# The last product of a down part, made in two matmuls of 256 columns

## The chip, the cores and the metric

The kernel runs on one core of a Trainium2 chip. The metric is device time in microseconds (us) of one execution. Engines are named as in the profile: PE is the matmul engine and PEld its loading of weights, DVE the vector engine, ACT the scalar engine, POOL GpSimd, SP the engine that issues most transfers.

## The reference

One decoder layer on 256 rows of 1024 columns in float32: a norm, attention with 16 heads of 64, a projection, a second norm, a gated feed-forward block with a causal convolution of width 3 (D_FF = 2816), a last norm. The change sits in the feed-forward block:

```python
def conv_ffn(y, w_up, conv_w, conv_b, w_down):
    u = y @ w_up
    u = causal_depthwise_conv(u, conv_w) + conv_b      # width 3, cut short here
    gate, val = jnp.split(u, 2, axis=-1)
    return (jax.nn.silu(gate) * val) @ w_down
```

## The kernel before, in words

Every float32 matrix is split in a high and a low part, `whi` (made by ACT, line 141) and `wlo` (made by DVE, line 154), and each product is made as three: high x high, low x high, high x low. All matmuls of these products go through one helper, `mm` on line 73, so the profile shows one line for them and tells them apart by their tiles.

The feed-forward block works on 22 tiles of 128 hidden columns. **An up tile** (`up`, `up_k`) makes 128 gate and 128 value columns for all 256 rows: 2 x 8 x 3 = 48 matmuls with a weight tile as the stationary operand and 256 columns of `yt` moving, written to a tile named `bank`. `gates` then reads the bank on DVE (line 540), runs the convolution and the gate on ACT and DVE, and leaves `at`, the 128 hidden columns split in high and low. **A down part** (`down`) multiplies two finished `at` tiles with 256 rows of `w_down`: `rows_product` is called for `kk` = 0 and 1, and each call goes over two halves of the rows (`t`), three products (`n`) and two halves of the output columns, 12 matmuls with `at` as the stationary operand and 512 columns of the weight moving. They add into four accumulators named `acc`, which stay open over all parts.

The order on PE is the order in which the code is written (the schedule is manual). From up tile 3 on, each odd up tile is followed by a down part, so PE runs 24 matmuls of 512 columns, then 96 of 256 (two up tiles), and so on. There are eight such down parts (0 to 7); after the last of them four up tiles follow, 192 matmuls. The three down parts that are left (`TAIL`) come after all up tiles; at the very end their last output columns are made in two banks of 256 columns (lines 642 to 649), with `at` stationary as in the other down parts.

```python
    def down(i, chains, whole=False):
        ...
        for kk in range(2):
            k = 2 * i + kk
            rows_product(accs, at[k], ("d", i), kk, chains, k == 0, ...)
```

The splits into `whi` and `wlo` run ahead of PE by a set number of pieces (`split_to`, `AHEAD`); DVE and ACT share their time between them and `gates`.

Of the kernel before, what the change touches and what calls it, by code (L numbers as in the profile page):

```python
# [16 lines left out]
NT = S // P  # L17
# [6 lines left out]
NF = F // P  # L24
# [14 lines left out]
def bucket_of(d):  # L39
    exact = BUCKETS // 2  # L40
    if d < exact:
        return d
    big = exact + int(math.log(d / exact) / math.log(MAX_DIST / exact) * (BUCKETS - exact))
    return min(big, BUCKETS - 1)
# [3 lines left out]
def tile_block(ctx: ExitStack, tc, x, attn_norm, w_qkv, w_o, rel_bias, ffn_norm, w_up, conv_w,  # L48
# [14 lines left out]
    def acc():  # L63
        return psA.tile([P, 512], F32, name="acc")
# [7 lines left out]
    def mm(o, lhsT, rhs, start, stop):  # L72
        nc.tensor.matmul(o, lhsT, rhs, start=start, stop=stop, skip_group_check=True)  # L73
# [92 lines left out]
    def split_to(g, ahead=0):  # L166
        n = 2 * (place[g] + 1) + ahead
        unit(max(0, n - state["lo"]))
# [114 lines left out]
    while d1 >= 0:  # L283
        b = bucket_of(d1)
# [3 lines left out]
        n = d1 - d0 + 1  # L288
# [12 lines left out]
    rk, rq = (ap.tile([P, S], F32, name=n) for n in ("rk", "rq"))  # L301
    nc.vector.memset(stat[:, 1, :], 0.0)

    def rows_product(accs, lhs, g, kk, chains, start, stop):

        for t in range(NT):
            halves = [half for half in range(2) if (t, half) in chains]
            a_hi, a_lo = (lhs[:, i, t * P:(t + 1) * P] for i in range(2))
            for n, (a, w) in enumerate(((a_hi, hi), (a_lo, hi), (a_hi, lo))):
                for half in halves:  # L310
                    mm(accs[t, half], a, w[g, kk][:, half * 512:(half + 1) * 512],
                       start and n == 0, (stop is True or stop == (t, half)) and n == 2)

    CHAINS = [(t, half) for t in range(NT) for half in range(2)]
    accs = {c: acc() for c in CHAINS}
# [3 lines left out]
    for i in range(4):  # L319
        if i < 3:  # L320
            transposed(2 * i + 2, g1)
        for kk in range(2):
            k = 2 * i + kk
            rows_product(accs, yt[:, :, k, :], ("v", i), kk, CHAINS, k == 0, k == KD - 1)
        unit(2)
        if i == 1:
            nc.scalar.activation(junk[0], xt[0], AF.Square, accum_out=stat[:, 0, 0:1])
        if i == 2:
            nc.scalar.activation(junk[1], xt[1], AF.Square, accum_out=stat[:, 0, 1:2])
            r1 = rstds()  # L330
            d1 = diagonals(r1)
# [119 lines left out]
    accs = {}  # L451

    def o_part(t, half, ks):
        if (t, half) not in accs:
            accs[t, half] = acc()
        for k in ks:
            split_to(("o", k // 2))
            rows_product(accs, ot[:, :, k, :], ("o", k // 2), k % 2, [(t, half)], k == 0, k == KD - 1)
# [50 lines left out]
    at = {}  # L509
    accs = {}  # L510
# [54 lines left out]
    def down(i, chains, whole=False):  # L565
        split_to(("d", i))
        for c in chains:
            if c not in accs:
                accs[c] = acc()
        for kk in range(2):  # L570
            k = 2 * i + kk
            rows_product(accs, at[k], ("d", i), kk, chains, k == 0, k == NF - 1 or (CHAINS[3] if whole and kk else False))

    first = [up_ps() for _ in range(2)]
    up_k(0, first[0], range(0, 4))
# [9 lines left out]
    for j in range(NF):  # L585
        if j < 2:
            gates(j, first[j])
        else:
            up(j)
        if j == 4:  # L590
            nc.scalar.activation(gf, gf, AF.Copy, scale=math.sqrt(D))
        split_to(("up", j), AHEAD if j < 8 else AHEAD + 2)
        i = (j - 3) // 2
        if j >= 3 and j % 2 == 1 and i < first_tail:
            down(i, CHAINS, i == first_tail - 1)
            split_to(("d", i), AHEAD if j < 8 else AHEAD + 2)
# [34 lines left out]
    for i in range(first_tail, NG - 1):  # L631
        down(i, CHAINS[:2])
    left, right = slice(0, 512), slice(512, D)
    down(NG - 1, [(0, 0)])
    add_part(0, left, 3, accs[0, 0])
    down(NG - 1, [(0, 1)])
# [44 lines left out]
```

## Time and profile before

| | |
|---|---|
| time, median of 3 runs | 319.25 us (319.23 to 319.75) |
| time of the profiled execution | 319.19 us |
| its span in the trace | 317.4 us |
| PE busy | 306.6 us (97%), 2142 matmuls |
| weight loads (PEld) | 280.9 us (89%) |
| DVE, ACT, POOL busy | 243.0, 180.2, 17.3 us |

The span runs from the first to the last instruction in the trace; the 1.8 us between it and the time lie around it. A busy PE in the profile is not a PE at its peak: matmuls overlap, and what the next one adds to the time is the distance from start to start, which the text calls the step of a matmul.

### The profile page before, as it was taken

To read this page: it belongs to the slowest core of one execution; us is meant where nothing else is said; L and a number is where in the kernel's file an instruction comes from. 1 tells how busy PE (TensorE), PEld (TensorE's weight loads), DVE (VectorE), ACT (ScalarE), POOL (GpSimd) and SP (SyncE) were. 2 spreads that over 40 slices of the span, in tenths; PEclk is the share of its full clock that TensorE was granted. 3 is DMA by queue.
4 is the path that set the end of the run, shared out by engine and by line. 5 is a ranking of instruction groups with operands and counts; after the bars stand their busy time and mean duration, and the time that the engine had idled before them with its cause. 6 is when DMAs were issued, how large, how long until landed. Compare 5 with 4: busy or idle time off the path is not lost.

```text
span 317.4 us, 5462 instructions
## 1 busy us (share of the span) xinstructions
PE 306.6 (97%) x2142; PEld 280.9 (89%) x2142; DVE 243.0 (77%) x460; ACT 180.2 (57%) x322; POOL 17.3 (5%) x55
## 2 busy tenths in 40 slices
PE   7999998999999999999999999999999999999992
PEld 7788998988888788999998989898989999999881
DVE  2475888888888595599988695989595959599662
ACT  4675576555556684557656464757272727366221
POOL 4602000000000000000000000000000000000000
PEclk9999999999999999999999999999999999999998
DMA  7997396718442356247476556567374747500011
GB/s 243 417 379 234 103 328 187 276 24 265 144 122 95 121 146 250 70 142 255 139 262 201 197 157 240 191 213 261 132 267 132 259 140 221 177 0 2 0 68 66
DMA packets 38902, 56.58 MB, mean 178 GB/s; under 512 B 1164, under 2 KB 32604, under 8 KB 38876
## 3 DMA queue, kind: packets, MB, share of 16 engines
q1 hardware_dynamic: 37724, 53.05, 49.0%
q0 software_dynamic: 848, 2.65, 3.1%
q10 hardware_dynamic: 304, 0.53, 0.4%
q8 instruction: 17, 0.28, 0.3%
q14 instruction: 9, 0.07, 0.1%
HBM read 55.15 MB, written 1.07 MB: 177 GB/s over the span
## 4 chain that ended last, share of the span: by engine, by line
PE 72%; ACT 9%; DVE 9%; issue 5%; DMA 3%; SPq 1%; POOLq 0%; POOL 0%; DVEq 0%; ACTq 0%
PE bank L73 41%; PE acc L73 29%; ACT sc L395 4%; DMA raw<-in_w_qkv_dram 3%; DVE sc L386 3%; ACT whi L141 2%; DVE wlo L154 2%; ACT ot L427 1%; ACT pt L411 1%; DVE pt L412 1%; DVE ot L429 1%; PE twobank L73 1%; DVE xs L608 0%; PE bank L258 0%; SPq L184 0%
## 5 line engine op out<-in xcount | busy, mean ns | idle before, releaser
L73 PE MATMUL bank<-yt,whi 128*128 128x256 f32 x720 | 127.1, 280 | 0.1
L154 DVE TENSOR_TENSOR wlo<-raw,whi 128x1024 fp32r<-128x1024 f32 x98 | 117.1, 1219 | 1.2 <-ACT whi L141 1.1
L73 PEld LDWEIGHTS bank<-yt,whi 128*128 128x128 f32 x720 | 110.2, 188 | 1.1 <-ACT yt L260 0.5
L73 PE MATMUL bank<-yt,wlo 128*128 128x256 f32 x360 | 100.8, 280 | 0.0
L141 ACT ACTIVATE whi<-raw 128x1024 fp32r<-128x1024 f32 x98 | 98.7, 1049 | 3.6 <-DMA raw<-in_w_qkv_dram 3.6
L73 PEld LDWEIGHTS bank<-yt,wlo 128*128 128x128 f32 x360 | 68.8, 191 | 0.0
L544 ACT ACTIVATE cv<-u,params 128x256 f32<-128x256 f32 x44 | 24.2, 598 | 69.0 <-DVE u L540 69.0
L73 PE MATMUL acc<-whi,at 128*128 128x512 f32 x164 | 44.7, 389 | 0.0
L73 PE MATMUL acc<-yt,whi 128*128 128x256 f32 x224 | 40.3, 283 | 0.0
L73 PEld LDWEIGHTS acc<-yt,whi 128*128 128x128 f32 x224 | 33.8, 188 | 2.4 <-issue 2.3
L73 PEld LDWEIGHTS acc<-whi,at 128*128 128x128 f32 x164 | 30.1, 188 | 5.7
L540 DVE TENSOR_TENSOR u<-bank,rb 128x512 f32<-128x512 f32 x22 | 15.2, 690 | 24.5 <-PE bank L73 24.4
L73 PE MATMUL acc<-yt,wlo 128*128 128x256 f32 x112 | 31.0, 277 | 0.0
L73 PE MATMUL acc<-wlo,at 128*128 128x512 f32 x82 | 26.1, 389 | 0.0
L395 ACT ACTIVATE sc<-sc,nm 128x128 f32<-128x128 f32 (+1 forms) x32 | 14.3, 448 | 19.2 <-DVE nm L390 19.2
L556 DVE SCALAR_TENSOR_TENSOR cv<-u,params,cv 128x254 f32<-128x254 f32 x44 | 21.3, 483 | 1.6
L554 DVE SCALAR_TENSOR_TENSOR cv<-u,params,cv 128x255 f32<-128x255 f32 x44 | 21.1, 479 | 0.3 <-ACT cv L544 0.3
L73 PEld LDWEIGHTS acc<-yt,wlo 128*128 128x128 f32 x112 | 21.0, 188 | 0.0
L73 PE MATMUL acc<-whi,ot 128*128 128x512 f32 x64 | 20.4, 397 | 0.4 <-DVE ot L429 0.4
L73 PEld LDWEIGHTS acc<-wlo,at 128*128 128x128 f32 x82 | 15.4, 188 | 3.2
L73 PE MATMUL acc<-whi,yt 128*128 128x512 f32 x64 | 17.6, 396 | 0.0
L73 PEld LDWEIGHTS acc<-whi,ot 128*128 128x128 f32 x64 | 11.6, 188 | 3.0 <-DVE ot L429 0.7
(119 smaller groups left out, 306.5 us busy)
## 6 DMA issues: line engine op xcount, KB each, us to landing
raw<-in_w_up_dram SPq DMA_DIRECT2D x22, 1024.0 KB, 5.1
raw<-in_w_qkv_dram SPq DMA_DIRECT2D x11, 1024.0 KB, 8.4
raw<-in_w_down_dram SPq DMA_DIRECT2D x11, 1024.0 KB, 4.9
raw<-in_w_o_dram SPq DMA_DIRECT2D x4, 1024.0 KB, 7.0
bias<-line_d POOLq DMA_DIRECT2D x8, 256.0 KB, 5.0
raw<-in_w_qkv_dram SPq DMA_DIRECT2D x2, 512.0 KB
xs<-in_x_dram SPq DMA_DIRECT2D x2, 256.0 KB
xs<-in_x_dram SPq DMA_DIRECT2D x1, 512.0 KB
```

Source lines behind the costliest of these rows:

```text
L73: nc.tensor.matmul(o, lhsT, rhs, start=start, stop=stop, skip_group_check=True)
L141: nc.scalar.activation(h, src, AF.Copy)
L154: nc.vector.tensor_tensor(l, src, h, op=ALU.subtract)
L386: nc.vector.tensor_tensor_reduce(out=sc[p][:, a, c], in0=ps[:, c], in1=bias[p][:, a, b], op0=ALU.add, op1=ALU.max, scale=1.0, scalar=-3.0e ...
L395: nc.scalar.activation(sc[p][:, a, c], sc[p][:, a, c], AF.Exp, bias=nm[:, j], accum_out=z[:, j])
L411: nc.scalar.activation(pt[p][:, 0, :], ps[:, :768], AF.Copy)
L412: nc.vector.tensor_tensor(pt[p][:, 1, :], ps[:, :768], pt[p][:, 0, :].bitcast(F32), op=ALU.subtract)
L427: nc.scalar.activation(h, o, AF.Copy)
L540: nc.vector.tensor_tensor(u, ps, rb2.unsqueeze(1).to_broadcast([P, 2, S]), op=ALU.mult)
L544: nc.scalar.activation(c[:, a, :], u[:, a, :], AF.Identity, scale=w2, bias=b)
L554: nc.vector.scalar_tensor_tensor(c[:, a, 1:], u[:, a, :S - 1], w1, c[:, a, 1:], op0=ALU.mult, op1=ALU.add)
L556: nc.vector.scalar_tensor_tensor(c[:, a, 2:], u[:, a, :S - 2], w0, c[:, a, 2:], op0=ALU.mult, op1=ALU.add)
```

## The change

`rows_product` gets an argument `border`. Where it is set, the last matmul of the call (second half of the rows, third product, second half of the output columns) is made as two matmuls of 256 columns, into the two halves of the same 512 columns of the accumulator, with the same stationary operand. `down` sets it for `kk` = 1 of the parts that make all four chains, which are the parts 0 to 7.

```diff
-    def rows_product(accs, lhs, g, kk, chains, start, stop):
+    def rows_product(accs, lhs, g, kk, chains, start, stop, border=False):
...
             for n, (a, w) in enumerate(((a_hi, hi), (a_lo, hi), (a_hi, lo))):
                 for half in halves:
-                    mm(accs[t, half], a, w[g, kk][:, half * 512:(half + 1) * 512],
-                       start and n == 0, (stop is True or stop == (t, half)) and n == 2)
+                    pieces = 2 if border and (t, n, half) == (NT - 1, 2, halves[-1]) else 1
+                    size = 512 // pieces
+                    for b in range(0, 512, size):
+                        mm(accs[t, half][:, b:b + size], a, w[g, kk][:, half * 512 + b:half * 512 + b + size],
+                           start and n == 0, (stop is True or stop == (t, half)) and n == 2)
...
-            rows_product(accs, at[k], ("d", i), kk, chains, k == 0, k == NF - 1 or (CHAINS[3] if whole and kk else False))
+            rows_product(accs, at[k], ("d", i), kk, chains, k == 0,
+                         k == NF - 1 or (CHAINS[3] if whole and kk else False), kk == 1 and chains == CHAINS)
```

On PE the end of down part 0 and the start of up tile 4 stand like this before (the names are output <- operands; `acc` marks the down part, `bank` the up tile; 128x256 and 128x512 are the outputs):

```order
L73 MATMUL acc<-whi,at 128x512 x4
L73 MATMUL acc<-wlo,at 128x512 x2
L73 MATMUL bank<-yt,whi 128x256 x2
L73 MATMUL bank<-yt,wlo 128x256
L73 MATMUL bank<-yt,whi 128x256 x2
```

And the same place in the changed kernel:

```order
L73 MATMUL acc<-whi,at 128x512 x4
L73 MATMUL acc<-wlo,at 128x512
L73 MATMUL acc<-wlo,at 128x256 x2
L73 MATMUL bank<-yt,whi 128x256 x2
L73 MATMUL bank<-yt,wlo 128x256
L73 MATMUL bank<-yt,whi 128x256 x2
```

The second of the two matmuls with `wlo` has become two of half the width, so the matmul ahead of the up tile has 256 columns where it had 512. The other seven places read alike; nothing else moves on PE, and the orders of DVE, ACT, POOL and SP are as before.

## Rows read from the trace of the kernel before

**Rows 1.** The page: busy time of the engines; PE and its granted clock in 40 slices of the span, in tenths; the chain that ended last, by line.

```profile
PE 306.6 (97%) x2142; PEld 280.9 (89%) x2142; DVE 243.0 (77%) x460; ACT 180.2 (57%) x322; POOL 17.3 (5%) x55
...
PE   7999998999999999999999999999999999999992
...
PEclk9999999999999999999999999999999999999998
...
PE bank L73 41%; PE acc L73 29%; ACT sc L395 4%; DMA raw<-in_w_qkv_dram 3%; DVE sc L386 3%; ACT whi L141 2%; DVE wlo L154 2%; ACT ot L427 1%; ACT pt L411 1%; DVE pt L412 1%; DVE ot L429 1%; PE twobank L73 1%; DVE xs L608 0%; PE bank L258 0%; SPq L184 0%
```

**Rows 2.** The chain that ended last, in order of time, in the feed-forward block: start in us, length in us, what, and how many instructions. `bank` pieces are up tiles, `acc` pieces down parts.

```profile
129.79 5.46 PE bank L73 x48
135.69 13.61 PE bank L73 x120
149.30 5.46 PE acc L73 x24
154.76 11.31 PE bank L73 x96
166.07 5.44 PE acc L73 x24
171.50 11.31 PE bank L73 x96
182.81 5.44 PE acc L73 x24
...
255.24 11.31 PE bank L73 x96
266.55 5.44 PE acc L73 x24
271.99 22.61 PE bank L73 x192
294.60 6.81 PE acc L73 x30
```

**Rows 3.** PE's instructions in order of time at the end of up tile 3 and the start of down part 0: start in us, time from the first start to the last end in us, engine, line, operation, output <- operands, shapes, how many of a kind in a row.

```profile
148.69 0.28 PE L73 MATMUL bank<-yt,wlo 128*128 128x256 f32 x1
148.80 0.39 PE L73 MATMUL bank<-yt,whi 128*128 128x256 f32 x2
149.03 0.28 PE L73 MATMUL bank<-yt,wlo 128*128 128x256 f32 x1
149.14 1.08 PE L73 MATMUL acc<-whi,at 128*128 128x512 f32 x4
150.06 0.62 PE L73 MATMUL acc<-wlo,at 128*128 128x512 f32 x2
```

**Rows 4.** The same view at the end of down part 0 and the start of up tile 4.

```profile
154.14 0.62 PE L73 MATMUL acc<-wlo,at 128*128 128x512 f32 x2
154.60 0.40 PE L73 MATMUL bank<-yt,whi 128*128 128x256 f32 x2
154.83 0.28 PE L73 MATMUL bank<-yt,wlo 128*128 128x256 f32 x1
154.95 0.40 PE L73 MATMUL bank<-yt,whi 128*128 128x256 f32 x2
155.19 0.28 PE L73 MATMUL bank<-yt,wlo 128*128 128x256 f32 x1
```

**Rows 5.** The same view at two other places where a run of 256-column matmuls begins: after the spread of the row factors (128-column matmuls into `acc`, ahead of the rest of up tile 1), and in attention after the scores (`bank<-kt,qt`).

```profile
135.19 0.50 PE L73 MATMUL acc<-diag,ones 128*128 128x128 f32 x3
135.44 0.48 PE L73 MATMUL bank<-yt,whi 128*128 128x256 f32 x2
135.77 0.28 PE L73 MATMUL bank<-yt,wlo 128*128 128x256 f32 x1
135.88 0.39 PE L73 MATMUL bank<-yt,whi 128*128 128x256 f32 x2
136.11 0.28 PE L73 MATMUL bank<-yt,wlo 128*128 128x256 f32 x1
...
57.78 0.50 PE L73 MATMUL acc<-yt,whi 128*128 128x256 f32 x2
58.12 0.29 PE L73 MATMUL acc<-yt,wlo 128*128 128x256 f32 x1
58.24 0.39 PE L73 MATMUL acc<-yt,whi 128*128 128x256 f32 x2
58.48 0.28 PE L73 MATMUL acc<-yt,wlo 128*128 128x256 f32 x1
58.59 0.39 PE L73 MATMUL acc<-yt,whi 128*128 128x256 f32 x2
58.81 0.28 PE L73 MATMUL acc<-yt,wlo 128*128 128x256 f32 x1
```

**Rows 6.** The same view near the end of the program, where the last output columns of the down parts go into a bank of 256 columns.

```profile
306.45 0.39 PE L73 MATMUL acc<-wlo,at 128*128 128x512 f32 x1
306.68 0.40 PE L73 MATMUL bank<-whi,at 128*128 128x256 f32 x2
306.91 0.28 PE L73 MATMUL bank<-wlo,at 128*128 128x256 f32 x1
307.03 0.40 PE L73 MATMUL bank<-whi,at 128*128 128x256 f32 x2
307.27 0.28 PE L73 MATMUL bank<-wlo,at 128*128 128x256 f32 x1
```

**Rows 7.** Busy time of each engine (and its instructions) in one stretch of 16.70 us, one down part and two up tiles, with granted clock, share of the DMA engines and GB/s; and who waited for whom between 155 and 306 us (us in total, times, longest in us).

```profile
core 0: us, PE busy (x) PEld busy (x) DVE busy (x) ACT busy (x) POOL busy (x), PEclk, DMA share, GB/s
221.60:238.30 16.70, 16.70 (x121) 15.80 (x120) 12.99 (x21) 9.08 (x16) 0.00 (x0) 1.00 0.56 190
...
ACT cv L544 <- DVE u L540: 60.6, 18, 5.6
DVE u L540 <- PE bank L73: 24.4, 17, 3.4
```

## The prediction

> **What bounds the kernel now.** I read the page first. PE is busy 97% of the span, its granted clock is full in every slice but the last, and the two largest pieces of the chain that ended last are PE's up tiles (41%) and PE's down and output products (29%) [rows 1]. So between 130 and 306 us only the step of the matmuls sets the time. The second view is the chain in order of time [rows 2]. The reader is to divide each length by its count:
>
> - up tiles ahead of the first down part: 13.61 us / 120 = 113.4 ns a matmul;
> - down parts: 5.44 us / 24 = 226.7 ns a matmul of 512 columns;
> - up tiles behind a down part: 11.31 us / 96 = 117.8 ns, and 22.61 us / 192 = 117.8 ns behind the last.
>
> The same code runs at two speeds, and the slower one begins with the first down part and never ends, not even across the border between two up tiles. The single instructions show it as well [rows 3, 4]: ahead of the first down part a matmul with `wlo` comes every 0.34 us (148.69, 149.03), three matmuls further on; behind it every 0.36 us by these rounded starts (154.83, 155.19), which by the chain's mean is 3 x 117.8 = 353 ns. It is not the clock: that is granted at 1.00, the 2.4 GHz level, in the slow stretch too [rows 7]. It is not a wait: PE is busy 16.70 of 16.70 us there.
>
> What does the speed hang on? On how a run of 256-column matmuls is entered, it seems. Behind 128-column matmuls the first step is long (the `wlo` row starts 0.33 us after the run does, 135.44 to 135.77, for two steps), and then the distance of the `wlo` rows is 0.34 us; after the scores it goes from 0.36 to 0.33 [rows 5]. Behind a matmul of 512 columns with no pause it starts at the slow step and stays (eight borders of this kind, the first in [rows 4]). At the end of the program there is a ninth entry from 512 columns, with other operands, and it stays slow too: 0.36 us for three, 120 ns each [rows 6]. The change puts two 256-column matmuls between the 512-column run and each of the eight slow runs.
>
> **The change part by part.**
>
> *What it adds.* Eight matmuls and eight weight loads, for the two halves of eight products. A half has not run behind a 512-column matmul with `wlo` in this place, so its step is bounded from rows: from below 113.4 ns [rows 2], where two halves cost as much as one whole (2 x 113.4 = 226.8 against 226.7 ns); from above the 120 ns of the same kind of operands at the end [rows 6], 13 ns more than a whole. Eight times that is 0 to 0.11 us; I take 0.05, the middle, since nothing in the rows is nearer to one end.
>
> *What it could give back.* Behind the eight borders stand 7 x 96 + 192 = 864 up matmuls. They take 7 x 11.31 + 22.61 = 101.78 us; at 13.61 / 120 us each, a figure that has the uneven first steps of one entry in it, they would take 97.99 us. The difference is 3.79 us. The bounds are nothing (the run stays slow) and 3.84 us (three matmuls in 0.340 us instead of 0.3533, 288 times).
>
> *What comes with it.* A down part behind a fast up tile starts with slower steps: the first one takes 5.46 us, the others 5.44 [rows 2]. Seven more parts and the run at the end would pay this, 8 x 0.02 = 0.16 us.
>
> *What could be late next.* If a down part and two up tiles take 5.46 + 96 x 0.1134 = 16.3 us instead of 5.44 + 11.31 = 16.75, DVE has to do its 12.99 us and ACT its 9.08 us in that [rows 7]: 80% and 56% of it. DVE waits for PE's banks 17 times in this stretch, 24.4 us in all, and not the other way round, so it has room, and the splits that feed PE go with it. I cost this at nothing; without that room the most that could be lost is the gain itself. The transfers run at 0.56 of the DMA engines there. No queue, wait or buffer is moved: the halves write the same accumulator, and an up tile's bank is freed by DVE as before.
>
> *The sum.* 319.19 us (the profiled execution; 0.06 below the median of the runs shown) - 3.79 + 0.05 + 0.16 = 315.6 us.
>
> **A rule against it.** The up run has one operand shape and two steps, 113.4 and 117.8 ns, and the 512-column step is 226.7 ns, just twice the faster [rows 2]. The Trainium skill, in "TensorE: Matmul & The Clock Gate", section "Back-to-back issue gap", gives one gap for each column count, N / 2.4 + 2.5 ns: 109.2 ns for 256 columns and 215.8 for 512. By that rule two halves cost 2.5 ns more than a whole, 0.02 us in all, and nothing that stands ahead of a matmul changes its step, so the time would stay. This trace differs with it in both: all three steps are longer, and one column count has two of them. It does not refute it in what matters here, namely that a half ahead of a run might do nothing for it.
>
> **The rivals.**
>
> *The slow step goes through the halves.* The first half is itself entered from 512 columns without a pause, just as the up tile is today, and the last rows show such a run staying slow with these very operands for as long as it lasts [rows 6]. The border would only have moved by two matmuls: 319.19 + 0 to 0.11 = 319.2 to 319.3 us. For it speaks that all nine entries from 512 columns stay slow. Against it speaks that the run at the end has another slow step (120 ns) than the up tiles (117.8), so the up matmuls meet another state than the one that a 512-column matmul leaves, and that the uneven entries, with steps of 120 ns and more, all end in the fast one [rows 5]. This is also the case that the rule above gives.
>
> *A slower step than now.* The up tiles take over the step that the halves bring along, 120 ns as in [rows 6], and keep it as they keep 117.8 now. It costs 864 x (120 - 117.8) = 1.9 us and gives 321.1 us. It decides from about 0.7 ns a matmul on, which is 0.6 us. For it speaks that a step once taken lasts for 192 matmuls; against it, that no run with these operands, fast or slow, shows 120 ns as its lasting step [rows 2].
>
> *Only some of it.* Some borders end fast, or the run falls back to the slow step later; half the gain gives 317.4 us. Against it: the eight borders have the same instructions, and the seven lengths of 11.31 us show no difference between them, so they should go one way together.
>
> **How the numbers follow.** The fast step has 0.52: most kinds of entry lead to it, and only one kind, which the change replaces, does not. Its own range is 315.2 to 316.0 us. The halves doing nothing have 0.31, part of the gain 0.07, a slower step 0.10. Within 0.2% (0.6 us) a run of this kernel cannot well be told from no change: its three times spread over 0.5 us. So faster has 0.52 + 0.07 = 0.59, same 0.31, slower 0.10. The range must leave out no more than 0.2: from 315.2 (all of the 3.84 us and a little run noise) to 319.6 (no gain, with the spread of the runs) it leaves out the slower step alone.
>
> **What would show it.** In the chain of the changed kernel the pieces of 96 up matmuls should be 10.9 us instead of 11.31, and the last of 192 some 21.8 instead of 22.61. The two halves should stand ahead of them with steps of 113 to 120 ns, and the down parts should be 0 to 0.03 us longer. DVE's wait for the banks should shrink and no wait of PE appear. If the 11.31 is still there, the step goes through the halves; 11.5 would be the slower step. If it is 10.9 but the time has not fallen by 3 us, PE waits somewhere for DVE, for the splits or for a transfer, and I have mis-sized the room.

## The result, and the profile after

The changed kernel takes 315.78 us, the kernel before 319.24 us (medians of six runs each); the ratio is 0.9891, with an interval of 0.9876 to 0.9906. Forecast were 315.6 us and a range of 315.2 to 319.6. The profiled execution of the changed kernel took 315.89 us, with a span of 314.1 us against 317.4.

The page of the changed kernel, busy times of the engines, as in [rows 1]:

```profile
PE 302.8 (96%) x2150; PEld 276.8 (88%) x2150; DVE 242.9 (77%) x460; ACT 179.9 (57%) x322; POOL 17.3 (6%) x55
```

Eight matmuls more (2150), and 3.8 us less of PE; DVE, ACT and POOL do the same work. The chain in order of time (start, length, what, how many) answers [rows 2]:

```profile
135.91 13.61 PE bank L73 x120
149.52 5.46 PE acc L73 x25
154.98 10.90 PE bank L73 x96
165.88 5.46 PE acc L73 x25
171.34 10.90 PE bank L73 x96
...
253.14 10.90 PE bank L73 x96
264.04 5.46 PE acc L73 x25
269.50 21.78 PE bank L73 x192
291.28 6.83 PE acc L73 x30
```

All seven pieces of 96 up matmuls have gone from 11.31 to 10.90 us, the last of 192 from 22.61 to 21.78: 113.5 ns a matmul, the step that the run ahead of the first part had already. PE's instructions at the end of part 0 answer [rows 4] (the two halves are in the `wlo` row, which names the first of its shapes):

```profile
154.36 0.62 PE L73 MATMUL acc<-wlo,at 128*128 128x512 f32 x3
154.82 0.40 PE L73 MATMUL bank<-yt,whi 128*128 128x256 f32 x2
155.06 0.28 PE L73 MATMUL bank<-yt,wlo 128*128 128x256 f32 x1
155.18 0.39 PE L73 MATMUL bank<-yt,whi 128*128 128x256 f32 x2
155.40 0.28 PE L73 MATMUL bank<-yt,wlo 128*128 128x256 f32 x1
155.52 0.39 PE L73 MATMUL bank<-yt,whi 128*128 128x256 f32 x2
155.74 0.28 PE L73 MATMUL bank<-yt,wlo 128*128 128x256 f32 x1
```

The reader is to look at the `wlo` rows: 155.06, 155.40, 155.74, that is 0.34 us for three matmuls. By the single starts in the trace the two halves take 113 and 119 ns, the first up steps 121, 122, 115, 115, and then it is 113.3.

The time adds up by pieces: the up runs 7 x 10.90 + 21.78 = 98.08 us instead of 101.78, so 3.70 less; the parts 8 x 5.46 instead of 5.46 + 7 x 5.44, so 0.14 more; the run behind the last up tile 6.83 instead of 6.81. The run ahead of part 0 began 0.22 us later in this execution (135.91 instead of 135.69 on the chain). That makes 3.32 us, and the spans differ by 3.3.

### The profile page after: what moved, and what is told of

Its sections match the earlier page's. It is cut to its first block, busy times and chain, and to the rows that moved or that the text cites. A ratio compares the mean times of both kernels' runs of the same rounds, so it can differ in the third digit from the quotient of the medians.

```text
span 314.1 us, 5478 instructions
## 1 busy us (share of the span) xinstructions
PE 302.8 (96%) x2150; PEld 276.8 (88%) x2150; DVE 242.9 (77%) x460; ACT 179.9 (57%) x322; POOL 17.3 (6%) x55
## 4 chain that ended last, share of the span: by engine, by line
PE 72%; ACT 9%; DVE 9%; issue 5%; DMA 3%; SPq 1%; POOLq 0%; POOL 0%; DVEq 0%; ACTq 0%
PE bank L73 40%; PE acc L73 29%; ACT sc L401 4%; DMA raw<-in_w_qkv_dram 3%; DVE sc L392 3%; ACT whi L141 3%; DVE wlo L154 2%; ACT ot L433 1%; ACT pt L417 1%; DVE pt L418 1%; DVE ot L435 1%; PE twobank L73 1%; DVE xs L615 0%; PE bank L258 0%; SPq L184 0%
## 5 line engine op out<-in xcount | busy, mean ns | idle before, releaser
L73 PE MATMUL bank<-yt,whi 128*128 128x256 f32 x720 | 123.4, 277 | 0.1
L73 PEld LDWEIGHTS bank<-yt,whi 128*128 128x128 f32 x720 | 108.5, 188 | 0.5 <-ACT yt L260 0.5
L73 PE MATMUL bank<-yt,wlo 128*128 128x256 f32 x360 | 99.4, 276 | 0.0
L73 PEld LDWEIGHTS bank<-yt,wlo 128*128 128x128 f32 x360 | 67.6, 188 | 0.0
L73 PE MATMUL acc<-wlo,at 128*128 128x512 f32 (+1 forms) x90 | 26.1, 370 | 0.0
L73 PEld LDWEIGHTS acc<-wlo,at 128*128 128x128 f32 x90 | 16.9, 188 | 3.5
```

## The experiments

Each is told with its up pieces, since the single times of one kernel lie up to 1.4 us apart (last section). The kernel before took 319.8 to 319.9 us on the chips that ran these (318.88 for the last one), so differences are given to the kernel before on the same chip. The cuts of code are against the changed kernel, except where the text says that no product is halved or that it is the kernel before.

**Where the halves stand.** Theory A: what stands directly ahead of the up run decides. Theory B: one more matmul and weight load does it. Theory C: a run of 512-column matmuls makes the next run slow only once it has settled to its own step.

The product ahead of the last one is halved:

```diff
-                    pieces = 2 if border and (t, n, half) == (NT - 1, 2, halves[-1]) else 1
+                    pieces = 2 if border and (t, n, half) == (NT - 1, 2, halves[0]) else 1
```

> The product ahead of the last one is halved instead of the last, so each part ends with 256, 256, 512 columns and the up run is again entered from a 512-column matmul. Theory A (the width of the matmul directly ahead of the up run decides): the up pieces stay at 11.31 us for 96, time 319.2 to 319.4 us. Theory B (one more matmul and weight load per part is what counts, wherever it stands): 10.90 us for 96, 315.8 us. Theory C (a 512-column matmul only makes the run slow once it has settled to its own step of 226.7 ns): the one 512-column matmul behind the halves has not settled, 10.90 us, 315.8 us.

Measured: 316.38 us, 3.5 us below the kernel before, ratio 0.9887 (0.9873 to 0.9902). The chain:

```profile
149.94 5.45 PE acc L73 x25
155.39 10.91 PE bank L73 x96
166.30 5.47 PE acc L73 x25
```

The up run is fast behind a 512-column matmul. Theory A is out. B and C stand.

The first of the last twelve products is halved, eleven of 512 columns follow:

```diff
-                    pieces = 2 if border and (t, n, half) == (NT - 1, 2, halves[-1]) else 1
+                    pieces = 2 if border and (t, n, half) == (0, 0, halves[0]) else 1
```

> The first of the last twelve products of each part is halved instead of the last; eleven products of 512 columns follow. Theory A: 11.31 us for 96 up matmuls, 319.2 to 319.4 us. Theory B: 10.90 us, 315.8 us. Theory C: the eleven have settled by the end (the first part settles within four or five), 11.31 us, 319.2 to 319.4 us.

Measured: 320.18 us, ratio 1.0007 (0.9998 to 1.0016).

```profile
150.02 5.47 PE acc L73 x25
155.49 11.31 PE bank L73 x96
166.80 5.47 PE acc L73 x25
```

The extra pair is there (x25), the gain is not: theory B, that one more matmul and weight load do it wherever they stand, is out. By the single starts the products behind the halves take 234, 236, 228, 232, 231 ns and then 227, so the run has settled when the up tile comes, as theory C has it.

Two further places test how far this reaches: the halved product has two, then four behind it (`(NT - 1, 1, halves[-1])` and `(NT - 1, 0, halves[-1])` in the same line).

> The product with two more behind it is halved, so a part ends with 256, 256, 512, 512 columns. Theory C with the settling that the parts show at their start (three steps of 231 to 232 ns, then 227): two products behind the halves have not settled, 10.90 us for 96, 3.5 us below the kernel before. If one step is enough to settle: 11.31 us, as the kernel before.

> The product with four more behind it is halved. Theory C with three steps to settle: the run has settled when the up tile begins, 11.31 us for 96, time as the kernel before (0 to 0.1 us above). If settling takes longer than at the parts' start, or if theory B holds within the last six products: 10.90 us, 3.5 us below the kernel before.

Measured: 315.50 and 315.85 us, one run each, 4.4 and 4.0 us below the kernel before; 10.90 and 10.89 us for 96. The second was a miss by my count of three steps to settle: its four products still take 234, 236, 228 and 232 ns. That the run had not settled, and that an extra matmul among the last six products is enough, say the same of this run, and no run with `at` in this place tells them apart. The chain with four behind:

```profile
149.38 5.48 PE acc L73 x25
154.86 10.89 PE bank L73 x96
```

The two halves taken apart (256, 512, 256 columns):

```diff
...
+                todo = [(half, 0, 512) for half in halves]
+                if border and (t, n) == (NT - 1, 2):
+                    todo = [(1, 0, 256), (0, 0, 512), (1, 256, 256)]
...
```

> The two halves are taken apart: the last products of a part are 256, 512, 256 columns. If the up run needs only an entry that has not settled (theory C, which the second-last product halved bore out): 10.90 us for 96, 3.5 us below the kernel before. If it needs two 256-column matmuls in a row somewhere behind the settled run: 11.31 us, as the kernel before.

Measured: 316.06 us in one run, 3.8 us below the kernel before; 10.89 us for 96. Two in a row are not needed.

**How long it lasts.** Halves at the border of part 0 only:

```diff
-                         k == NF - 1 or (CHAINS[3] if whole and kk else False), kk == 1 and chains == CHAINS)
+                         k == NF - 1 or (CHAINS[3] if whole and kk else False), kk == 1 and chains == CHAINS and i == 0)
```

> Halved at the border of part 0 only. If the step lasts until the next run of 512 columns and no longer: the first piece of 96 takes 10.90 us, the other six 11.31 and the last of 192 takes 22.61, time 319.2 - 0.4 = 318.8 us. If one such entry is enough for the rest of the program: 315.8 us.

Measured: 319.50 us, ratio 0.9983 (0.9971 to 0.9995), 0.36 us below the kernel before; 0.4 were expected.

```profile
149.93 5.45 PE acc L73 x25
155.38 10.90 PE bank L73 x96
166.27 5.46 PE acc L73 x24
171.73 11.31 PE bank L73 x96
183.03 5.44 PE acc L73 x24
```

The step holds to the next down part and no longer; each border has to be paid and is worth 0.41 us by itself (11.31 - 10.90).

**Does it have to be halves?** No product halved, and one matmul of two constants, 128 columns wide, behind each part:

```diff
             down(i, CHAINS, i == first_tail - 1)
+            mm(two_banks()[:, :P], ones, ident, True, True)
```

> The products are left whole; behind each of the eight parts stands one matmul of two constants, 128 columns, into a bank of its own that nothing reads. Theory that any uneven entry leads to the fast step: 10.90 us for 96 as with the halves, plus some 0.1 to 0.2 us for each of the eight extra matmuls, 316.6 to 317.4 us. Theory that the halves work by their own operands or by their weight load: 11.31 us stay and the extra matmuls come on top, 320.0 to 320.8 us.

Measured: 317.97 us, 1.9 us below the kernel before, ratio 0.9937 (0.9922 to 0.9952).

```profile
149.99 5.44 PE acc L73 x24
155.43 0.22 PE twobank L73 x2
155.65 10.90 PE bank L73 x96
166.55 5.45 PE acc L73 x24
```

Fast at all eight borders, at 0.22 us for each extra matmul (the trace shows it as two, x2) where two halves cost 5 ns. So it is not the halves' operands. The time lies above the 316.6 to 317.4 us that were expected, which was reckoned from 319.2 us; against the kernel before on this chip 1.8 to 2.6 us less were expected, and 1.9 is the dear end of that, since 8 x 0.22 = 1.8 us. Not every interruption does it: in this same trace the up run ahead of part 0 keeps its slow step through four 128-column matmuls (14.13 us for 120, from 135.85 us on).

The last product cut in 384 and 128 columns:

```diff
...
+                    todo = [(0, 0, 512), (1, 0, 384), (1, 384, 128)]
...
```

> The last product is cut in 384 and 128 columns instead of two of 256. If any uneven step is enough: 10.90 us for 96; the 128-column piece may wait for its weight load (some 110 ns instead of 57), so 8 x 0.05 = 0.4 us more than the changed kernel, 3.1 us below the kernel before. If the halves work because they are of the up run's own width: 11.31 us, 0.4 us above the kernel before.

Measured: 315.84 us in one run, 4.0 us below the kernel before; 10.95 us for 96; by the starts the two pieces take 171 and 60 ns and the first up step 170. The 0.05 us that was expected of the 128-column piece came at the first up step instead. Equal widths are not needed.

**What the operands have to do with it.** Every product of the eight parts in two halves. (This kernel does not compute the reference: in part 0 each half of a first product opens its sum anew. Only its steps are read.)

```diff
-                    pieces = 2 if border and (t, n, half) == (NT - 1, 2, halves[-1]) else 1
+                    pieces = 2 if border else 1
...
-                         k == NF - 1 or (CHAINS[3] if whole and kk else False), kk == 1 and chains == CHAINS)
+                         k == NF - 1 or (CHAINS[3] if whole and kk else False), chains == CHAINS)
```

> Every product of the parts 0 to 7 is made in two of 256 columns, 48 in a part. They are entered from a fast up run. If matmuls of the down parts' operands take the fast step as well: 48 x 113.4 = 5.44 us a part, up pieces of 10.90 us, 3.5 us below the kernel before. If they only have the 120 ns step: 5.76 us a part, 8 x 0.3 = 2.4 us more than the changed kernel, 1.1 us below the kernel before; the up runs behind them 10.90 us if a run of 120 ns steps is an unsettled entry, and 11.31 us or 96 x 120 = 11.5 us if the slow step is passed on.

Measured: 317.98 us in one run, 1.8 us below the kernel before.

```profile
149.38 5.74 PE acc L73 x48
155.12 10.90 PE bank L73 x96
166.02 5.74 PE acc L73 x48
```

5.74 us / 48 = 120 ns, entered from a fast up run: with these operands 120 ns is the lasting step. And it isn't handed on, the up runs behind it are fast.

The changed kernel with the ninth entry halved too, ahead of the banks at the end of the program:

```diff
-                         k == NF - 1 or (CHAINS[3] if whole and kk else False), kk == 1 and chains == CHAINS)
+                         k == NF - 1 or (CHAINS[3] if whole and kk else False), kk == 1 and (chains == CHAINS or (i == NG - 1 and chains == [(1, 0)])))
```

> The changed kernel, and in addition the last product ahead of the two 256-column banks at the end of the program is halved (the ninth entry from a settled 512-column run). If the entry decides there as at the eight borders: the 36 matmuls at the end go from 120 ns to 113.4 ns, 35 x 6.6 = 0.23 us less than the changed kernel, 3.5 + 0.2 = 3.7 us below the kernel before. If these operands (the weight moving, the two at parts stationary) have only the 120 ns step: as the changed kernel, 3.5 us below the kernel before.

Measured: 316.42 us, ratio 0.9899 (0.9877 to 0.9921), 3.4 us below the kernel before. The instructions there answer [rows 6]:

```profile
302.96 0.40 PE L73 MATMUL bank<-whi,at 128*128 128x256 f32 x2
303.20 0.28 PE L73 MATMUL bank<-wlo,at 128*128 128x256 f32 x1
303.32 0.28 PE L73 MATMUL bank<-whi,at 128*128 128x256 f32 x1
```

From the bank's second matmul on the starts lie 120 ns apart as before (303.20, 303.32): no gain. In these runs the entry decides only where both steps have been seen for the operands as they lie.

What gives a run its steps? The kernel before with `yt` and everything allocated behind it moved by 64 bytes against the weight tiles:

```diff
-    act.tile([P, 48], F32, name="skew")
+    act.tile([P, 64], F32, name="skew")
```

> The kernel before with nothing changed but an unused tile ahead of yt, 64 columns in place of 48, which moves yt and all that is allocated behind it by 64 bytes against the weight tiles. Theory that the slow step depends on where operands lie against each other: the up pieces leave 11.31 us for 96, either way, or the 120 ns step at the end changes. Theory that only the order of the matmuls makes it: 11.31 us and 120 ns as before, time as the kernel before.

Measured: 324.45 us in one run, 4.6 us above the kernel before. The chain:

```profile
136.95 14.39 PE bank L73 x120
151.34 5.60 PE acc L73 x24
156.94 11.50 PE bank L73 x96
```

And PE's instructions at the end of the program:

```profile
312.33 0.28 PE L73 MATMUL bank<-wlo,at 128*128 128x256 f32 x1
312.45 0.39 PE L73 MATMUL bank<-whi,at 128*128 128x256 f32 x2
312.67 0.28 PE L73 MATMUL bank<-wlo,at 128*128 128x256 f32 x1
```

All the steps have changed. The up runs take 120 ns (14.39 / 120, 11.50 / 96) behind 128-column matmuls and behind a part alike, at a granted clock of 1.00, the parts 233 ns instead of 227, and the matmuls at the end 0.34 us for three, 113 ns, where they had 120. So the steps that a run can take depend on where its operands lie. Whether the place of the moved tiles counts by itself or only against the weight tiles, this run does not tell, nor does the next: both change together.

Last, only `at` is moved by 64 bytes, `yt` and the weights lie as before:

```diff
+    fp.tile([P, 16], F32, name="skew")
     gf = fp.tile([P, D], F32, name="gf")
```

> The kernel before, no product halved, with an unused tile of 16 columns ahead of the feed-forward tiles: at lies 64 bytes further against the weights, yt and the weights lie as before. Theory that each run's step comes from how its own two operands lie against each other, as moving both yt and at suggested: the parts take 5.60 us as there and the 256-column matmuls at the end 113.5 ns. Theory C then says that a 512-column run that never gets to its 226.7 ns step leaves the up runs fast without any halves: 10.90 us for 96, in all 3.8 us less for the up runs, 1.3 us more for eight parts, 0.4 us more and 0.2 us less at the end, 2.3 us below the kernel before. If the slow up step comes from the 512-column matmul's width and not from its settling: 11.31 us, 1.4 us above the kernel before.

Measured: 319.62 us, the kernel before on that chip 318.88, one run each: 0.7 us above, between the two that were expected.

```profile
150.01 5.60 PE acc L73 x24
155.61 10.89 PE bank L73 x96
...
172.09 11.31 PE bank L73 x96
183.40 5.60 PE acc L73 x24
189.00 10.90 PE bank L73 x96
...
205.49 11.31 PE bank L73 x96
...
272.29 22.62 PE bank L73 x192
```

The parts take 5.60 us and the matmuls at the end 113.5 ns, as expected from the place of `at` alone. Theory C is half right: the parts never get to 227 ns here (by the single starts most of their steps go between 231 and 236 ns, 233 in the mean), and yet the up runs behind them are fast and slow by turns, four of each. That the 512-column matmuls are not at 227 ns is not enough for the 113 ns step; both steps follow them.

The single starts show one thing that goes with the outcome in all traces with `yt` in its old place. Where an up run stands directly behind a whole 512-column product, the distance from the start of that product to the first up matmul is 226 to 230 ns at all 27 entries that lead to the 118 ns step (229 and 230 with `at` moved) and 232 to 236 ns at all 28 that lead to the 113 ns step. Whether it is a cause or a sign of one was not tested.

## Why the prediction was right, step by step

*One shape, two steps, and the entry decides.* Borne out for the up tiles with `yt` and `at` where they lie. Over these traces, every up run behind a 512-column run that had settled to 227 ns was slow (the eight of before, eight with the halves eleven products ahead, seven of the kernel with one border): 23 of 23. Every one behind a cut product with at most four products behind it, behind a part made of halves, or behind the extra 128-column matmul was fast: 73 of 73. The transfers do not set the step here: in the kernel before it is 117.8 ns in the first up run behind a part, with the DMA engines busy to 0.92 (155 to 165 us), and in the last, with 0.14 (271.9 to 294.6 us), at a granted clock of 1.00 in both.

*"The uneven entries all end in the fast one."* This step was wrong. It rested on entries of one trace. The up run after the spread of the row factors, which [rows 5] shows fast, takes 14.13 us instead of 13.61 in the trace with the second-last product halved (its row stands in the last section), 117.8 ns, though nothing ahead of it had been changed. The kernel with `at` moved shows it again, behind the parts. The forecast came out because at these eight borders the halves do lead to the fast step, not because every uneven entry does; that they were of the kind that does was luck. What else in the state at the entry decides is open; no experiment got at it.

*The gain.* 3.79 us forecast, 3.70 measured (3.84 was the bound). The price of the halves: 113 + 119 - 227 = 5 ns each, 0.04 us; 0.05 was taken. The slower start of the parts: 0.16 forecast; the parts and the run at the end together cost 0.14 + 0.02 us with the halves in them, so 0.12 by itself. The prediction lets the matmuls set the time up to 306 us; the chain leaves PE at 301.4 us (294.60 + 6.81 in [rows 2]), and no term of the sum hangs on the difference.

*The room of DVE and ACT.* As costed. Who waited for whom between 155 and 303 us in the changed kernel (us in total, times, longest):

```profile
DVE u L546 <- PE bank L73: 21.1, 8, 3.2
```

And a stretch of one part and two up tiles, columns as in [rows 7]:

```profile
218.00:234.36 16.36, 16.36 (x123) 15.45 (x122) 13.03 (x22) 9.11 (x16) 0.00 (x0) 1.00 0.55 193
```

The stretch is 0.34 us shorter, DVE does its 13.0 us in it, it still waits for PE, and PE is busy throughout at a granted clock of 1.00.

*The rivals.* That the slow step goes through the halves: ruled out, with its argument from [rows 6]. With that run's operands, where they lie, no lasting step but 120 ns came up (the ninth entry halved, and the parts in halves), so it said nothing of the up tiles. The slower step: 120 ns does last with the parts' operands, as feared, but the up runs behind it are fast. Part of the gain only: no border differed from the others.

*The rule from the Trainium skill.* In "TensorE: Matmul & The Clock Gate", section "Back-to-back issue gap", N / 2.4 + 2.5 ns (an estimate of 109.2 for 256 columns) is the gap of a single matmul; for a stream of weight loads and matmuls, which is what runs here, the Trainium skill says there that both set the spacing, and it gives 131 ns for 512 columns. The prediction took the first for the rule of a stream. The runs agree with neither: 227 ns at best for 512 columns, and 113, 118 and 120 ns for the same 128x128 by 256 shape. The measured steps decide, and the difference between two of them is nearly the whole effect of this change.

## What to carry to other kernels

When a matmul-bound kernel shows one shape at two steps, divide the chain's pieces by their counts, run by run, and look at where the step changes; a cut of one product where the longer step begins, which cost 5 ns here, is worth a try, at every border again. Ask also where the operands lie: moving a tile by 64 bytes cost or gave 2 to 6% of a step here, and can help one run while it harms another. And before a rule of entry is drawn from one trace, look at the same entry in a second one.

## What the runs showed of the hardware that I had not expected

- The place of operands sets which steps come up. With `yt` as in the kernel before, up runs have 113.4 or 117.8 ns; with it and all behind it 64 bytes further, 120 ns only. `at` as before: 227 ns for 512 columns and 120 ns for 256; 64 bytes further, 233 and 113.5 ns.
- A 512-column run has a settling of its own: behind two halves its steps are 234, 236, 228, 232, 231 and then 227 ns.
- The up matmuls ahead of part 0 run fast in one trace and slow in another. In the thirteen traces with `yt` in its old place they were fast in seven, as in [rows 2] (5.46 + 13.61 = 19.07 us for 168), and slow in six. The chain of the kernel with the second-last product halved shows the same two pieces, 128-column matmuls between them:

```profile
129.70 5.66 PE bank L73 x48
135.80 14.13 PE bank L73 x120
```

That is 19.79 us, 0.72 more, and the slow step is kept through the interruption. The runs of one kernel scatter by as much and more (319.04 to 319.78 us before, 315.50 to 316.68 after, 318.64 to 320.01 with one border). That this is their cause was not shown: each kernel left one trace, so it is open whether the step there goes by the kernel or by the execution.
